# Turning the attention weights of the first two query groups on VectorE and carrying them by DMA, in a stick-breaking decoder block

## The chip, the cores and the metric

The kernel runs on one core of a Trainium2 chip. The metric is the device time of one execution in microseconds, as the median over runs. The profile is of one execution; its own time is given beside its span, which is the stretch from the first to the last instruction. All data is 32-bit floating point. A product of two 32-bit numbers is made from parts: a high part (the number rounded to the format that TensorE multiplies, `float32r`) and a low part (what the rounding left), and of the four products of parts the one of the two low parts is dropped.

## The reference

One decoder layer for one sequence of 1024 tokens and a width of 1024, with 16 heads of 64. What matters here:

```python
h = rms_norm(x, norm_gain) * (1 + scale) + shift           # scale, shift, gate from c
q, k, v, z_a, u, z_b, m_a, m_b = split(h @ w_in)           # 8 x 1024 columns
# stick-breaking attention: key s of query t, s < t
z = q @ k.T * 64 ** -0.5
w = sigmoid(z) * prod_{s < j < t} (1 - sigmoid(z_tj))
attn = w @ v
p_a = (attn * silu(z_a)) @ w_branch_a
p_b = (pool(u) * silu(z_b)) @ w_branch_b                   # window means minus the token
out = rms_norm(x + gate * ((sigmoid(m_a) * p_a + sigmoid(m_b) * p_b) @ w_out))
```

## The kernel before

The sequence is stored backwards, so that the keys a query may see are those after it, and a running product from left to right gives the stick-breaking weights. The program has five stages, one after another: the modulation, the norm and the projection `u`; the values `v` (written to DRAM as `v_d`); the pooling branch with `wzb`, `pool` and `pb`; the attention, with the remaining projections `p` in between; and the end, with `pa` and `o`.

Weights of `w_in` come in tiles of 128 columns: 40 of them belong to the attention stage (`tiles`). Of the first 8 (`PLAIN`) the low part is made where they are used, with the copy on ScalarE and the subtraction on GpSimd. Of the other 32 it is made early by `make_lo` (L129): a load `l_raw`, a copy on ScalarE (L136), a subtraction on VectorE (L137), a store to `wl_d`. `LO_V` and `LO_PB` say how many are made per step of the values and of the pooling branch.

**Attention.** The heads come in 8 pairs `p` of heads `h`; the queries of a head come in 4 groups `t` of 256, each of two blocks `qb` of 128. A unit is (p, h, t); `HT_ORDER` gives the eight units of a pair: t = 0, 2, 0, 2, 1, 3, 1, 3 with h = 0, 0, 1, 1, 0, 0, 1, 1. For one unit:

- `z_items` (L531): for each block of queries, the scores `z` of 128 queries against W = 1024 − 128·qb keys, queries on the partitions, in chunks of at most 512 keys. ScalarE makes `om` (L550) and `be` (L551), GpSimd masks the diagonal (L555), VectorE makes the running product (the scan, L557) and multiplies it into `be` (L558). `be` then holds the weights.
- `turn` (L562): `be` has queries on the partitions, and the product with the values needs keys there. TensorE turns squares of 128 by 128 into a PSUM tile `wt`, up to four at a time (a chunk `kp`), ScalarE copies the high part out (L576), VectorE subtracts for the low part (L577).
- `product` (L580): `avs`, the values times the turned weights, high and low part in turn.
- `finish` (L594): the two halves of the result are added (L602, L603) and multiplied with the silu of z_a on GpSimd (L606), and stored to `ga_d`.

Per pair there are 72 squares to turn. TensorE's order is written out by hand: `step` (L653) deals a unit's product, the scores of the unit three steps ahead (`LEAD`) and 8 or 9 pieces of three `p` products evenly over one step, and TensorE keeps that order. A chunk is turned two chunks ahead of its product (`DEPTH`). The order of the other engines and of the queues is made by a scheduler that plays the program through with costs of its own; once made it is fixed, and an engine that waits for one instruction holds back all that stand behind it. SyncE (SP) issues nearly all DMAs, in its own fixed order. Eight semaphores are dealt round to the DMAs, and a DMA waits until the one before it on its semaphore has landed.

Of the kernel before, what the change touches and what calls it, by code (L numbers as in the profile page):

```python
# [9 lines left out]
F32 = mybir.dt.float32  # L10
# [15 lines left out]
LEAD = {0: 3, 1: 3, 2: 3, 3: 3}  # L26
NBE = (4, 4)
SHARE = (7,) * 8
# [4 lines left out]
BANKS = {"pj": 2, "z": 3, "av": 1, "tr": 2}  # L33
NWT = 4


PLAIN = 8
LO_V = (1, 1, 1, 1, 1, 1, 1, 0)
LO_PB = (1, 1, 1, 1, 1, 1, 2, 2)
HD = 64  # L40
# [8 lines left out]
def block_kernel(ctx, tc, a, out):  # L49
# [66 lines left out]
    def load_w(src, name, hi_eng, lo_eng):  # L116
        raw = wts.tile([P, KB, P], F32, tag="raw", bufs=2, name=name + "_raw")
        nc.sync.dma_start(raw.rearrange("p k c -> p (k c)"), src)
        return split(raw, [P, KB, P], wts, "whl", 2, hi_eng, lo_eng, name)
# [20 lines left out]
    def load_parts(i, name):  # L140
        if i < PLAIN:
            return load_w(a["w_in"][tiles[i]], name, act, gp)
        raw = wts.tile([P, KB, P], F32, tag="raw", bufs=2, name=name + "_raw")
# [42 lines left out]


    early = ExitStack()
    first = early.enter_context(pool("first"))
    with pool("init") as init:  # L190
# [74 lines left out]
        def first_w(i):  # L265
            raw = wts.tile([P, KB, P], F32, tag="raw", bufs=2, name=f"wu{i}_raw")
# [63 lines left out]
    with pool("vp") as vp:  # L330
        def load_wv(hf, k2):
            raw = wts.tile([P, 2, 512], F32, tag="raw", bufs=2, name=f"wv{hf}_{k2}_raw")
            nc.sync.dma_start(raw.rearrange("p k c -> p (k c)"), a["w_v"][hf, k2])
            return split(raw, [P, 2, 512], vp, "wv", 6, act, v, f"wv{hf}_{k2}")
# [31 lines left out]
    with pool("pb") as pb:  # L366
# [4 lines left out]
        for g, win in enumerate(WINDOWS):  # L371
            dhl = []
            for cb in range(2):
# [16 lines left out]
                dhl.append(split(d, [P, S], pb, "dhl", 3, v, v, f"dhl{j}"))  # L390
            praw = wts.tile([P, 2, 256], F32, tag="raw", bufs=2, name=f"praw{g}")
            nc.sync.dma_start(praw, a["pool_w"][g].rearrange("(k p) d -> p k d", p=P))
# [24 lines left out]
        for j in range(KB):  # L417
            sm = [pb.tile([P, 512], F32, tag="zs", bufs=3, name=f"sm{j}_{sh}") for sh in range(2)]
            whl = load_w(a["w_branch_b"][j], f"wb{j}", v, gp)
            wg = wts.tile([P, D], F32, tag="raw", bufs=2, name=f"wg{j}")  # L420
            nc.sync.dma_start(wg, a["w_gate"][j * P:(j + 1) * P, :])
# [17 lines left out]


    with pool("at") as at:
        pair = {}

# [43 lines left out]
        def projections():  # L487
# [7 lines left out]
            todo += gates  # L495
            ws = {}

# [33 lines left out]
        def z_items(u):  # L531

            p, h, t = u
            st = pair[p]
            rows = unit_rows[u] = []
            for qb in (2 * t, 2 * t + 1):
                n0 = qb * P
                W = S - n0
                om = at.tile([P, S], F32, tag="om", bufs=2, name=f"om{p}_{h}_{qb}")
                g = t // 2  # L540
                be = at.tile([P, S - 512 * g], F32, tag=f"be{g}", bufs=NBE[g], name=f"be{p}_{h}_{qb}")
                nch = (W + 511) // 512
                b0 = 0
                for i in range(nch):
# [11 lines left out]
                    if i == nch - 1:  # L556
                        v.tensor_tensor_scan(om[:, :W], om[:, :W], om[:, :W], 1.0, ALU.mult, ALU.min)  # L557
                        v.tensor_mul(be[:, 1:W], be[:, 1:W], om[:, :W - 1])  # L558
                        rows.append(be)
                    yield  # L560

        def turn(u, kp):  # L562

            p, h, t = u
            rows, k0 = unit_rows[u], 2 * t
            pt = bank("tr", f"wt{p}_{h}_{t}_{kp}")
# [13 lines left out]
        def product(u, kp, wt, blocks):  # L580

            p, h, t = u
            vv = pair[p]["vv"]
            if kp == t:
                i = units.index(u) % 2
                avs[u] = av_bank[:, 256 * i:256 * i + 256]
            for j, (kb, o, n) in enumerate(blocks):
                for i in range(2):
                    mm(
                        avs[u][:, :n], vv[:, kb, h].rearrange("p a d -> p (a d)"), wt[:, i, o:o + n],  # L590
                        start=kp == t and j == 0 and i == 0, stop=kp == 3 and j == 1 and i == 1,
                    )

        def finish(u):  # L594
# [9 lines left out]
            if h == 1:  # L604
                sl = slice(t * 256, t * 256 + 256)
                gp.tensor_mul(tp, tp, pair[p]["za"][:, sl])  # L606
                nc.sync.dma_start(ga_d[p][:, sl], tp)
            if (h, t) == HT_ORDER[-1]:
# [75 lines left out]

    with pool("fin") as fin:
        NK = 20

# [140 lines left out]
```

## Time and profile before

| what | value |
|---|---|
| median of 3 runs | 1292.53 us (1291.13 to 1293.98) |
| the profiled execution | 1294.87 us, span 1293.2 us |
| granted TensorE clock, mean | 0.99 |
| TensorE busy | 1241.9 us (96%) |
| VectorE busy | 804.1 us (62%) |
| ScalarE, GpSimd busy | 548.1 us (42%), 279.3 us (22%) |
| moved by DMA | 192.48 MB, mean 149 GB/s |

By the windows and the timeline the stages are: values 137.5 to 224 us; pooling branch to 431.6; attention to 1091, of which pairs 1 to 6 take about 75.4 us each; the end to 1293.2. A busy time is the union of an engine's records, so it hides which wait ends last; the timeline of one engine, with the starts of neighbouring rows, tells what an instruction costs the engine that issues it.

### The profile page before, as it was taken

The numbers are of one execution on the slowest core, as the hardware profiler recorded it, in microseconds if no ns is written. First come the engines' busy times: TensorE is split into PE (matmuls) and PEld (weight loads), VectorE is DVE, ScalarE is ACT, GpSimd is POOL, SyncE is SP. The second block draws the span as 40 slices with busy tenths as digits, with TensorE's granted clock in tenths as the row PEclk, the third lists the DMA queues.
The fourth block names the chain that finished last, engine by engine and source line by source line (L and its number), as shares of the span: only waits on it lengthen the run. The fifth ranks groups of instructions, "written<-read, shape, count | busy, mean of one in ns | idle before, by whom it ended". The sixth has DMA issues, their size and how long they took to land.

```text
span 1293.2 us, 16723 instructions
## 1 busy us (share of the span) xinstructions
PE 1241.9 (96%) x6094; PEld 1035.6 (80%) x6094; DVE 804.1 (62%) x1020; ACT 548.1 (42%) x1029; POOL 279.3 (22%) x397
## 2 busy tenths in 40 slices
PE   6799999989999999999999999999999998889997
PEld 5688888768888888888888888888888887667886
DVE  7915342899611177785877768686776743657654
ACT  4445331231101255565656556565655543312101
POOL 4610000102122332322313122231212211400001
PEclk9899999999999999999999999999999999899999
DMA  8528995862343411233323223232322237855512
GB/s 317 204 98 310 330 343 188 303 225 83 113 146 130 155 42 53 70 114 107 122 77 101 80 98 119 90 122 89 99 72 96 96 107 266 288 186 172 183 65 94
DMA packets 72804, 192.48 MB, mean 149 GB/s; under 512 B 7697, under 2 KB 21009, under 8 KB 70802
## 3 DMA queue, kind: packets, MB, share of 16 engines
q1 hardware_dynamic: 63106, 174.38, 39.4%
q10 hardware_dynamic: 9616, 17.04, 3.9%
q8 instruction: 48, 0.79, 0.2%
q14 instruction: 34, 0.28, 0.1%
HBM read 136.86 MB, written 50.34 MB: 145 GB/s over the span
## 4 chain that ended last, share of the span: by engine, by line
PE 78%; DVE 10%; issue 5%; DMA 4%; ACT 1%; POOL 1%; SPq 0%; POOLq 0%; DVEq 0%; ACTq 0%
PE p L90 30%; PE pb L90 7%; PE v L90 7%; PE avs L90 5%; PE o L90 5%; PE wzb L90 5%; PE z L90 5%; PE wt L90 4%; PE u L90 4%; PE pa L90 4%; DVE acc L234 2%; PE ua L90 1%; PE pool L90 1%; DMA wor<-in_w_out 1%; DVE om L557 1%
## 5 line engine op out<-in xcount | busy, mean ns | idle before, releaser
L90 PE MATMUL p<-hT,w 128*128 128x512 f32 x1920 | 538.2, 401 | 0.0
L90 PEld LDWEIGHTS p<-hT,w 128*128 128x128 f32 x1920 | 335.3, 189 | 45.9 <-issue 0.5
L557 DVE TENSOR_TENSOR_SCAN om<-om 128x512 f32<-128x512 f32 (+7 forms) x128 | 175.7, 1372 | 65.7 <-POOL om L555 41.1
L577 DVE TENSOR_TENSOR wt<-wt,wt 128x512 fp32r<-128x512 f32 (+1 forms) x160 | 101.1, 633 | 66.7 <-ACT wt L576 65.4
L550 ACT ACTIVATE om<-z 128x512 f32<-128x512 f32 (+2 forms) x192 | 94.3, 491 | 112.4 <-PE z L90 109.9
L555 POOL TENSOR_SCALAR_AFFINE_SELECT om<-om 128x128 f32<-128x128 f32 x128 | 62.0, 484 | 354.8 <-ACT om L550 318.1
L576 ACT CAST wt<-wt 128x512 fp32r<-128x512 f32 (+1 forms) x160 | 87.2, 545 | 74.9 <-PE wt L90 71.0
L90 PEld LDWEIGHTS avs<-wt,vv 128*128 128x128 f32 x640 | 96.0, 188 | 18.6 <-DVE tp L603 6.7
L558 DVE TENSOR_TENSOR be<-be,om 128x511 f32<-128x511 f32 (+7 forms) x128 | 102.4, 800 | 11.0
L90 PE MATMUL pa<-ga,wa 128*128 128x512 f32 x384 | 94.6, 402 | 10.9 <-DVE ga L698 3.9
L90 PE MATMUL avs<-wt,vv 128*128 128x256 f32 (+1 forms) x640 | 99.8, 278 | 4.5 <-DVE tp L603 4.5
L90 PEld LDWEIGHTS pa<-ga,wa 128*128 128x128 f32 x384 | 73.4, 194 | 31.0 <-DVE ga L698 5.2
L551 ACT ACTIVATE be<-z 128x512 f32<-128x512 f32 (+2 forms) x192 | 93.5, 487 | 0.0
L90 PE MATMUL wzb<-hT,wzb 128*128 128x512 f32 x384 | 92.2, 396 | 0.0
L90 PE MATMUL o<-wo,mhl 128*128 128x512 f32 (+1 forms) x408 | 89.6, 377 | 2.5 <-DVE mhl L114 2.5
L90 PEld LDWEIGHTS wt<-ident,be 128*128 128x128 f32 x576 | 72.4, 141 | 23.6 <-DVE wt L577 1.7
L90 PE MATMUL wt<-ident,be 128*128 128x128 f32 x576 | 89.1, 272 | 0.8 <-DVE wt L577 0.8
L90 PE MATMUL pb<-gb,wb 128*128 128x512 f32 x384 | 88.1, 391 | 0.0
L90 PE MATMUL v<-wv,hT 128*128 128x512 f32 x384 | 87.2, 389 | 0.0
L90 PEld LDWEIGHTS o<-wo,mhl 128*128 128x128 f32 x408 | 73.3, 188 | 17.3 <-DVE mhl L114 3.3
L90 PEld LDWEIGHTS wzb<-hT,wzb 128*128 128x128 f32 x384 | 73.1, 191 | 16.3 <-DVE zs L400 0.3
L90 PEld LDWEIGHTS pb<-gb,wb 128*128 128x128 f32 x384 | 72.1, 188 | 15.8
(118 smaller groups left out, 1538.9 us busy)
## 6 DMA issues: line engine op xcount, KB each, us to landing
w_raw<-in_w_in SPq DMA_DIRECT2D x40, 512.0 KB, 4.4
l_raw<-in_w_in SPq DMA_DIRECT2D x32, 512.0 KB, 5.5
wl_d<-l_raw SPq DMA_DIRECT2D x32, 512.0 KB, 5.0
w<-wl_d SPq DMA_DIRECT2D x32, 512.0 KB, 3.7
v_d<-vo SPq DMA_DIRECT2D x16, 512.0 KB, 5.3
vv<-v_d SPq DMA_DIRECT2D x8, 1024.0 KB, 5.7
wa_raw<-in_w_branch_a SPq DMA_DIRECT2D x16, 512.0 KB, 4.5
wa<-in_w_mod SPq DMA_DIRECT2D x7, 1024.0 KB, 5.5
```

Source lines behind the costliest of these rows:

```text
L90: ins = op(*args, **kw)
L234: v.scalar_tensor_tensor(acc, wa[:, k], sc[:, k:k + 1], acc, ALU.mult, ALU.add)
L550: act.activation(om[:, b0:b0 + n], zp[:, :n], AF.Sigmoid, scale=-0.125)
L551: act.activation(be[:, b0:b0 + n], zp[:, :n], AF.Sigmoid, scale=0.125)
L555: gp.affine_select(out=tl[:, :P], in_=tl[:, :P], pattern=[[1, P]], compare_op=ALU.is_gt, fill=fill, base=0, channel_multiplier=-1)
L557: v.tensor_tensor_scan(om[:, :W], om[:, :W], om[:, :W], 1.0, ALU.mult, ALU.min)
L558: v.tensor_mul(be[:, 1:W], be[:, 1:W], om[:, :W - 1])
L576: act.copy(wt[:, 0, :off], pt[:, :off])
L577: v.tensor_sub(wt[:, 1, :off], pt[:, :off], wt[:, 0, :off].bitcast(F32))
```

## The change

For units with t = 0 or 1 (`MOVED`) TensorE no longer turns the weights. VectorE turns each `be` in squares of 32 by 32 (one instruction per block of queries, `v.transpose`, 64 in all), into a tile `turned` of which there is one. Sixteen DMAs of 32 partitions each then carry the squares to the partitions where they belong, from SBUF to SBUF, into `moved` (two of them). `take` replaces `turn`: the copy of the high part and the subtraction read `moved` in SBUF instead of PSUM. The columns of `moved` stand in another order, so `product` reads them and writes `avs` with strides, in the same number of products, and the two halves of the result come out swapped, so `finish` multiplies and stores them in two pieces.

The other edits: `PLAIN` is 12 instead of 8, so 28 low parts are made early instead of 32: 8 with the values instead of 14, 12 in the pooling branch instead of 10. The raw weights get pools of their own, with 1 buffer in the attention stage and 2 at the end, where there were 2 throughout; the first two tiles of the attention are loaded ahead of its pool; `wt` has 3 buffers instead of 4, `be` of the turned units 2 instead of 4.

```diff
+NRAW = {1: 2, 2: 1, 3: 2}
+NWT = 3
+MOVED = (0, 1)
-PLAIN = 8
-LO_V = (1, 1, 1, 1, 1, 1, 1, 0)
-LO_PB = (1, 1, 1, 1, 1, 1, 2, 2)
+PLAIN = 12
+LO_V = (1, 0, 1, 0, 1, 0, 1, 0)
+LO_PB = (1, 1, 1, 1, 2, 2, 2, 2)
...
+    first_ws = {i: load_parts(i, f"w{tiles[i]}_{i}") for i in range(2)}
+    rest.close()
     with pool("at") as at:
+        raws.append(at)
...
+            if t in MOVED:
+                nr = 32 * (15 - 4 * t)
+                turned = at.tile([P, 4, 480], F32, tag="turned", bufs=1, name=f"turned{p}_{h}_{t}")
             for qb in (2 * t, 2 * t + 1):
...
                         v.tensor_tensor_scan(om[:, :W], om[:, :W], om[:, :W], 1.0, ALU.mult, ALU.min)
                         v.tensor_mul(be[:, 1:W], be[:, 1:W], om[:, :W - 1])
-                        rows.append(be)
+                        if t in MOVED:
+                            b1 = qb - 2 * t
+                            dst = turned[:, :, :nr].rearrange("p j (b c) -> p b j c", c=32)[:, b1::2]
+                            v.transpose(dst, be[:, :W].rearrange("p (b j c) -> p b j c", j=4, c=32))
+                        else:
+                            rows.append(be)
                     yield
+            if t in MOVED:
+                wm = at.tile([P, 4, 480], F32, tag="moved", bufs=2, name=f"moved{p}_{h}_{t}")
+                for i in range(4):
+                    for j in range(4):
+                        nc.sync.dma_start(wm[32 * j:32 * j + 32, i, :nr], turned[32 * i:32 * i + 32, j, :nr])
+                rows.append(wm)
+
+        def take(u, kp):
+            p, h, t = u
+            off, n = (0, 96) if kp == t else (96 + 128 * (kp - t - 1), 128)
+            wm = unit_rows[u][0]
+            wt = at.tile([P, 2, 4, 128], F32R, tag="wt", bufs=NWT, name=f"wt{p}_{h}_{t}_{kp}")
+            act.copy(wt[:, 0, :, :n], wm[:, :, off:off + n])
+            v.tensor_sub(wt[:, 1, :, :n], wm[:, :, off:off + n], wt[:, 0, :, :n].bitcast(F32))
...
+                    if t in MOVED:
+                        b0 = 2 - n // 32
+                        dst = avs[u].rearrange("p (b i c) -> p i b c", b=2, c=32)[:, :, b0:]
+                        mov = wt[:, i, :, o:o + n].rearrange("p i (b c) -> p i b c", c=32)
```

The change moves instructions on every engine of the attention stage. Three places follow. In the names, the first three numbers behind `om`, `be`, `turned` are pair, head and block of queries (for `turned` and `wt`, the group t); `SCALAR_TENSOR_TENSOR` on `om` is the scan.

**Place A, VectorE.** Head 1 of pair 3 makes its weights for group 0 while the unit (3, 0, 0) waits for its product. Before:

```order
L557 SCALAR_TENSOR_TENSOR om3_1_0_5651<-om3_1_0_5651 128x1024
L558 TENSOR_TENSOR be3_1_0_5652<-be3_1_0_5652,om3_1_0_5651 128x1023
L603 TENSOR_TENSOR tp2_3_5532<-avs_3008,tp2_3_5532 64x256
L557 SCALAR_TENSOR_TENSOR om3_1_1_5696<-om3_1_1_5696 128x896
L558 TENSOR_TENSOR be3_1_1_5697<-be3_1_1_5697,om3_1_1_5696 128x895
L476 TENSOR_TENSOR kl0_3002<-p12_1_5679,kh_4_5589 64x512
L577 TENSOR_TENSOR wt3_0_0_2_5748<-wt3_0_0_2_5743,wt3_0_0_2_5748 128x512
```

With the change:

```order
L570 SCALAR_TENSOR_TENSOR om3_1_0_5702<-om3_1_0_5702 128x1024
L571 TENSOR_TENSOR be3_1_0_5703<-be3_1_0_5703,om3_1_0_5702 128x1023
L648 TENSOR_TENSOR tp2_3_5571<-avs_2998,tp2_3_5571 64x256
L570 SCALAR_TENSOR_TENSOR om3_1_1_5743<-om3_1_1_5743 128x896
L571 TENSOR_TENSOR be3_1_1_5744<-be3_1_1_5744,om3_1_1_5743 128x895
L484 TENSOR_TENSOR kl0_2992<-p12_1_5725,kh_4_5641 64x512 x2
L576 STREAM_TRANSPOSE turned3_1_0_5701<-be3_1_0_5703 128x8x4x32
L576 STREAM_TRANSPOSE turned3_1_0_5701<-be3_1_1_5744 128x7x4x32
L595 TENSOR_TENSOR wt3_0_0_0_5679<-moved3_0_0_5591,wt3_0_0_0_5679 128x4x96
```

Before, the subtractions of chunks 0 and 1 of the unit (3, 0, 0) stand ahead of the first of these rows, and here only that of chunk 2. Now that of chunk 0 stands behind both scans, two subtractions for `kl` and both turns of the next unit.

**Place A, TensorE.** The same place in the order that is written by hand. Before:

```order
L90 MATMUL z3_1_1_1_5724<-kl1_3003,q1_3_5054 128x384
L90 MATMUL p12_1_5679<-hT_88,w12_16_5417 128x512 x6
L90 MATMUL wt3_0_0_2_5743<-ident_77,be3_0_0_5471 128x128
L90 MATMUL wt3_0_0_2_5743<-ident_77,be3_0_1_5512 128x128
L90 MATMUL wt3_0_0_2_5743<-ident_77,be3_0_0_5471 128x128
L90 MATMUL wt3_0_0_2_5743<-ident_77,be3_0_1_5512 128x128
L90 MATMUL avs_3008<-wt3_0_0_0_5631,vv_3_5420 128x256 x2
```

With the change:

```order
L93 MATMUL z3_1_1_1_5771<-kh_3_4896,q1_3_5091 128x384
L93 MATMUL z3_1_1_1_5771<-kl1_2993,q1_3_5091 128x384
L93 MATMUL p12_1_5725<-hT_88,w12_16_5463 128x512 x6
L93 MATMUL avs_2998<-wt3_0_0_0_5679,vv_3_5466 128x4x2x32 x2
L93 MATMUL avs_2998<-wt3_0_0_0_5679,vv_3_5466 128x128 x2
```

The four turns are gone, and six `p` products are what is left between the last scores of (3, 1, 0) and the first product of (3, 0, 0).

**Place C, VectorE.** The unit (2, 1, 1), while pair 3 begins. Before:

```order
L577 TENSOR_TENSOR wt2_1_1_1_5454<-wt2_1_1_1_5450,wt2_1_1_1_5454 128x384
L603 TENSOR_TENSOR tp2_1_5464<-avs_3008,tp2_1_5464 64x256
L577 TENSOR_TENSOR wt2_1_1_2_5489<-wt2_1_1_2_5484,wt2_1_1_2_5489 128x512
L485 TENSOR_TENSOR za_3_5421<-p27_0_5423,za_3_5421 128x512
L557 SCALAR_TENSOR_TENSOR om3_0_0_5470<-om3_0_0_5470 128x1024
L558 TENSOR_TENSOR be3_0_0_5471<-be3_0_0_5471,om3_0_0_5470 128x1023
```

With the change:

```order
L493 TENSOR_TENSOR za_3_5467<-p27_0_5469,za_3_5467 128x512
L570 SCALAR_TENSOR_TENSOR om3_0_0_5513<-om3_0_0_5513 128x1024
L571 TENSOR_TENSOR be3_0_0_5514<-be3_0_0_5514,om3_0_0_5513 128x1023
L648 TENSOR_TENSOR tp2_3_5571<-avs_2998,tp2_3_5571 64x256
L576 STREAM_TRANSPOSE turned3_0_0_5512<-be3_0_0_5514 128x8x4x32
L570 SCALAR_TENSOR_TENSOR om3_0_1_5550<-om3_0_1_5550 128x896
L595 TENSOR_TENSOR wt2_1_1_1_5496<-moved2_1_1_5405,wt2_1_1_1_5496 128x4x96
```

The subtraction of (2, 1, 1) moved from ahead of the scores of (3, 0, 0) to behind both of their scans and one turn.

More of the change, by code (lines that the diff above doesn't have):

```diff
@@ L26 @@
 LEAD = {0: 3, 1: 3, 2: 3, 3: 3}
-NBE = (4, 4)
+NBE = 4
 SHARE = (7,) * 8
@@ L116, in load_w @@
     def load_w(src, name, hi_eng, lo_eng):
-        raw = wts.tile([P, KB, P], F32, tag="raw", bufs=2, name=name + "_raw")
+        raw = raws[-1].tile([P, KB, P], F32, tag="raw", bufs=NRAW[len(raws)], name=name + "_raw")
         nc.sync.dma_start(raw.rearrange("p k c -> p (k c)"), src)
@@ L142, in load_parts @@
             return load_w(a["w_in"][tiles[i]], name, act, gp)
-        raw = wts.tile([P, KB, P], F32, tag="raw", bufs=2, name=name + "_raw")
+        raw = raws[-1].tile([P, KB, P], F32, tag="raw", bufs=NRAW[len(raws)], name=name + "_raw")
         nc.sync.dma_start(raw.rearrange("p k c -> p (k c)"), a["w_in"][tiles[i]])
@@ L185, in copy_out @@
         return use
+    rest = ExitStack()
+    raws = [rest.enter_context(pool("raw"))]
     early = ExitStack()
@@ L265, in first_w @@
         def first_w(i):
-            raw = wts.tile([P, KB, P], F32, tag="raw", bufs=2, name=f"wu{i}_raw")
+            raw = raws[-1].tile([P, KB, P], F32, tag="raw", bufs=NRAW[len(raws)], name=f"wu{i}_raw")
             load(raw.rearrange("p k c -> p (k c)"), a["w_in"][CU + i])
@@ L331, in load_wv @@
         def load_wv(hf, k2):
-            raw = wts.tile([P, 2, 512], F32, tag="raw", bufs=2, name=f"wv{hf}_{k2}_raw")
+            raw = raws[-1].tile([P, 2, 512], F32, tag="raw", bufs=NRAW[len(raws)], name=f"wv{hf}_{k2}_raw")
             nc.sync.dma_start(raw.rearrange("p k c -> p (k c)"), a["w_v"][hf, k2])
@@ L390, in block_kernel @@
                 dhl.append(split(d, [P, S], pb, "dhl", 3, v, v, f"dhl{j}"))
-            praw = wts.tile([P, 2, 256], F32, tag="raw", bufs=2, name=f"praw{g}")
+            praw = raws[-1].tile([P, 2, 256], F32, tag="raw", bufs=NRAW[len(raws)], name=f"praw{g}")
             nc.sync.dma_start(praw, a["pool_w"][g].rearrange("(k p) d -> p k d", p=P))
@@ L419, in block_kernel @@
             whl = load_w(a["w_branch_b"][j], f"wb{j}", v, gp)
-            wg = wts.tile([P, D], F32, tag="raw", bufs=2, name=f"wg{j}")
+            wg = raws[-1].tile([P, D], F32, tag="raw", bufs=NRAW[len(raws)], name=f"wg{j}")
             nc.sync.dma_start(wg, a["w_gate"][j * P:(j + 1) * P, :])
@@ L604, in finish @@
             if h == 1:
-                sl = slice(t * 256, t * 256 + 256)
-                gp.tensor_mul(tp, tp, pair[p]["za"][:, sl])
-                nc.sync.dma_start(ga_d[p][:, sl], tp)
+                n = 128 if t in MOVED else 256
+                for c0 in range(0, 256, n):
+                    c1 = t * 256 + (256 - n - c0)
+                    gp.tensor_mul(tp[:, c0:c0 + n], tp[:, c0:c0 + n], pair[p]["za"][:, c1:c1 + n])
+                    nc.sync.dma_start(ga_d[p][:, c1:c1 + n], tp[:, c0:c0 + n])
             if (h, t) == HT_ORDER[-1]:
```

17 lines of the change are left out of this document (12 added, 5 removed).

## Prediction

> **What bounds the kernel now.** I read the windows by stage first, because a busy share over the whole span mixes stages. The columns are stretch, length, PE busy, PEld, DVE, ACT, POOL, granted clock, DMA share, GB/s. The rows are the values stage, the start of the pooling branch, and pairs 2 and 3 of the attention:
>
> ```profile
> 137.50:222.00 84.50, 84.50 (x375) 69.96 (x374) 32.62 (x35) 26.95 (x33) 5.26 (x18) 1.00 0.83 296
> 250.00:266.00 16.00, 9.02 (x37) 6.29 (x36) 15.97 (x21) 6.00 (x8) 3.26 (x1) 1.00 0.71 235
> 607.00:682.00 75.00, 74.98 (x412) 63.86 (x411) 55.48 (x70) 45.84 (x95) 19.42 (x37) 1.00 0.34 109
> 682.00:757.00 75.00, 74.65 (x410) 63.47 (x409) 55.52 (x70) 44.78 (x94) 18.84 (x36) 1.00 0.30 95
> ```
>
> TensorE is never idle in the values stage and nearly never in the attention (74.98 and 74.65 of 75 us). Only the start of the pooling branch is VectorE's (15.97 of 16 us, TensorE 9.02). So work taken from TensorE in the attention shortens it, as long as nothing there arrives late. VectorE has room by this view: 55.5 of 75 us.
>
> Second, TensorE's timeline, for what a turn costs it (start, length, engine, line, operation, count). Two steps of one pair, each with a group of turns and a gap between two groups of `p` without one:
>
> ```profile
> 614.05 0.60 PE L90 MATMUL wt<-ident,be 128*128 128x128 f32 x4
> 614.40 0.95 PE L90 MATMUL p<-hT,w 128*128 128x512 f32 x3
> 615.19 0.39 PE L90 MATMUL z<-kh,q 128*128 128x512 f32 x1
> ...
> 617.48 0.49 PE L90 MATMUL wt<-ident,be 128*128 128x128 f32 x3
> 617.73 0.94 PE L90 MATMUL p<-hT,w 128*128 128x512 f32 x3
> 618.51 0.64 PE L90 MATMUL avs<-wt,vv 128*128 128x256 f32 x4
> 618.98 0.85 PE L90 MATMUL p<-hT,w 128*128 128x512 f32 x3
> 619.67 0.33 PE L90 MATMUL z<-kh,q 128*128 128x384 f32 x1
> ```
>
> Lengths of neighbours overlap, so I use distances between starts. Three `p` products alone take 619.67 − 618.98 = 0.69 us. With a group of four ahead of them it is 615.19 − 614.05 = 1.14, with three 618.51 − 617.48 = 1.03. A group of four costs 0.45 us, a group of three 0.34. (The records of these turns sum to far more, since they overlap other work.)
>
> **What the change removes.** For t = 0 and 1, a unit has 15 or 11 squares, three in its first group and four in each other: per pair 10 groups of four and 4 of three, 52 of 72 squares. 10 × 0.45 + 4 × 0.34 = 5.86 us per pair, **46.9 us** in 8 pairs. If nothing waited, that would be the gain.
>
> **What it adds on VectorE.** Per pair 2 × (1024 + 896 + 768 + 640) columns to turn, in eight instructions. The trace has no turn on VectorE. Its bounds for 1024 columns are a copy and a scan, and between them lies an operation that gives one result per column:
>
> ```profile
> L114 DVE CAST wzb<-wzb_raw 128x1024 fp32r<-128x1024 f32 x8 | 5.5, 687 | 1.2 <-DMA wzb_raw<-in_w_in 1.2
> L557 DVE TENSOR_TENSOR_SCAN om<-om 128x1024 f32<-128x1024 f32 x16 | 36.7, 2295 | 13.4 <-ACT om L550 12.8 <-POOL om L555 0.5
> L558 DVE TENSOR_TENSOR be<-be,om 128x1023 f32<-128x1023 f32 x16 | 20.3, 1271 | 2.0
> L577 DVE TENSOR_TENSOR wt<-wt,wt 128x384 fp32r<-128x384 f32 x64 | 35.4, 553 | 30.0 <-ACT wt L576 29.6
> ```
>
> The ends are 0.69 and 2.29 us. I take 1.2 for 1024 columns, near the 1.27 of L558, since a turn gives each element once; 1.05 for 896 and 0.9 for 768 in proportion. Per pair that is 3328 × 2 / 1024 × 1.2 = 7.8 us, so VectorE has some 63 us to do while TensorE keeps about 69. **By throughput the change would pay. The order decides otherwise.** The Trainium skill, page "VectorE: DVE Perf Modes", speaks against it twice: § The three transpose paths gives VectorE 311 ns for 128 by 128 and § Rules for kernel authors sends a square of that size to TensorE if PSUM will do. By that figure 1024 columns would take an estimated 8 × 311 = 2.49 us, above the scan of this trace, and the sum below would end near 1349; no run here shows it yet.
>
> **Place A, once in each pair.** The order rows above show the subtraction of chunk 0 of (3, 0, 0) behind both scans and both turns of (3, 1, 0), while TensorE has six `p` products between the last scores of (3, 1, 0) and the products that need this chunk. The same place in the trace of before, on three engines:
>
> ```profile
> 705.63 0.35 PE L90 MATMUL z<-kl,q 128*128 128x384 f32 x1
> 705.81 1.56 PE L90 MATMUL p<-hT,w 128*128 128x512 f32 x6
> 707.21 0.60 PE L90 MATMUL wt<-ident,be 128*128 128x128 f32 x4
> 707.56 0.65 PE L90 MATMUL avs<-wt,vv 128*128 128x256 f32 x4
> ...
> 706.01 0.49 ACT L550 ACTIVATE om<-z 128x384 f32<-128x384 f32 x1 [0.73 <-PE z L90]
> ...
> 706.87 2.02 DVE L557 TENSOR_TENSOR_SCAN om<-om 128x896 f32<-128x896 f32 x1
> 709.03 1.35 DVE L558 TENSOR_TENSOR be<-be,om 128x895 f32<-128x895 f32 x1
> 710.30 0.67 DVE L476 TENSOR_TENSOR kl<-p,kh 64x512 fp32r<-64x512 f32 x1
> 711.00 0.58 ACT L475 CAST kh<-p 64x512 fp32r<-64x512 f32 x1 [0.46 <-DVE kl L476]
> 712.73 0.69 DVE L476 TENSOR_TENSOR kl<-p,kh 64x512 fp32r<-64x512 f32 x1
> ```
>
> Without the turns TensorE could begin the products at 707.21. The chain that must end first runs from the scores: ScalarE is done at 706.50, then scan 2.02, multiplication 1.35, turns 1.20 and 1.05, subtraction 0.55 (L577, same size): 712.67. That is 5.5 us late. In pair 3 both `kl` subtractions (0.67, 0.69) and the copy that the second waits for (0.58) stand in between too: 7.4. In pairs 6 and 7 the rows of the order have one of the two turns ahead: 4.4. In the other five one or two `kl` subtractions stand within the chain, partly in its gaps: 6.0. Mean (7.4 + 2 × 4.4 + 5 × 6.0) / 8 = **5.8 us**, with ends 5.2 (no `kl` counts) and 7.0 (both and the copy count in six pairs). Nothing can cover it: TensorE's order is pinned, so everything behind stands still, the scores of the next units too. That delays their chains equally and gives nothing back.
>
> **Place C, seven times.** The subtraction of (2, 1, 1) stands behind both scans and one turn of (3, 0, 0):
>
> ```profile
> 687.25 0.35 PE L90 MATMUL z<-kl,q 128*128 128x384 f32 x1
> ...
> 688.83 0.60 PE L90 MATMUL wt<-ident,be 128*128 128x128 f32 x4
> ...
> 691.12 0.57 PE L90 MATMUL avs<-wt,vv 128*128 128x256 f32 x4
> ...
> 688.34 2.00 DVE L557 TENSOR_TENSOR_SCAN om<-om 128x896 f32<-128x896 f32 x1
> 690.48 1.09 DVE L558 TENSOR_TENSOR be<-be,om 128x895 f32<-128x895 f32 x1
> ```
>
> The products would begin 0.45 earlier than now, at 690.67. The scan ended at 690.34; with a turn of 1.2 ahead of it and the subtraction behind, 692.09: 1.4 late (pairs 1, 2, 5). In two pairs a subtraction for `za` (0.69 as for `kl`) is in between: 2.1; in two the multiplication instead of it: 690.34 + 1.20 + 1.09 + 0.55 = 693.18, 2.5 late. Mean (3 × 1.4 + 2 × 2.1 + 2 × 2.5) / 7 = 1.9, ends 1.4 and 2.5; I take **1.8**, as VectorE is free of three old subtractions just before.
>
> **Place B, once in each pair.** Products wait already for the sum of the group before:
>
> ```profile
> L90 PEld LDWEIGHTS avs<-wt,vv 128*128 128x128 f32 x640 | 96.0, 188 | 18.6 <-DVE tp L603 6.7
> ```
>
> That addition (L603) stands behind the scan of (p, 0, 1) in VectorE's order, and now behind its turn of 768 columns as well: **0.9 us**, ends 0 (the addition slips ahead) and 1.7 (at the scan's rate).
>
> **The carry.** A moved unit issues 16 DMAs; with eight semaphores the second eight wait for the first. Rows by issue, and one issue on SP:
>
> ```profile
> kh<-kh ACTq DMA_DIRECT2D x32, 128.0 KB, 3.6
> ga_d<-tp SPq DMA_DIRECT2D x32, 128.0 KB, 1.8
> 624.28 0.32 SPq L607 DMA_DIRECT2D ga_d<-tp  x1
> ```
>
> `kh<-kh` is the nearest, SBUF to SBUF. Sixteen issues take 5.1 us, two landings 3.6 (at 1.8) to 7.2 (at 3.6). They overlap, so I estimate the squares 7 to 10 us after the turn. A pair of 75 us has eight steps of 9.4 us; the product comes two steps after the unit's last scores, 18.8 us, of which the chain of place A takes 7, and the subtraction needs them 11 us after the turn or later. So the carry costs 0. That cover is gone at a landing of 6 us: two of them and the last eight issues make 14.6 us, 3.6 too late. SP's other DMAs (`w`, `vv`, `ga_d`) stand behind these sixteen. The loads of weights are issued a tile ahead and lose 5 us of some 19, so 0. The 16 extra `ga_d` stores and multiplications are read only in the end stage: 0.
>
> **The other edits.** In the values stage fewer low parts are made, but TensorE was the bound there, and the work removed ran beside it (VectorE 32.62 of 84.50 us): 0. The pooling branch makes two more, and its start is VectorE's:
>
> ```profile
> L137 DVE TENSOR_TENSOR l_raw<-l_raw,l_hi 128x1024 fp32r<-128x1024 f32 x32 | 39.9, 1245 | 41.4 <-ACT l_hi L136 41.3
> ```
>
> Two of 1.25 us: between 0 (they come in later steps, by `LO_PB`) and 2.5; I take 1. Four tiles more take the GpSimd way in the attention, where POOL is busy 19 of 75 us: 0. The smaller pools let the end's raw weights load later. The last `p` products hide it, and TensorE needs no weights of the end until then:
>
> ```profile
> 1075.74 15.89 PE L90 MATMUL p<-hT,w 128*128 128x512 f32 x69
> ```
>
> 0, with 3 us at most.
>
> **The sum.** 5.8 × 8 + 1.8 × 7 + 0.9 × 8 = 66.2 us of waits against 46.9 saved: +19.3 in the attention, +1 in the pooling branch. From the profiled execution's 1294.87 this is 1315.2. That execution lies 2.3 us above the median of 1292.53, so I forecast **1313 us**, slower by 1.6%. Its own range: low 5.2 × 8 + 1.4 × 7 + 7.2 − 46.9 = +11.7, so 1304; high 7.0 × 8 + 2.5 × 7 + 7.2 − 46.9 + 2.5 + 3 = +39, so 1332.
>
> **The rivals.**
>
> *VectorE runs ahead and place A is absorbed* (faster). It has about 12 us free in each pair. Were the scheduler's order only a tie there, that is, the scan able to start early enough, A would vanish and only C and B stay: 1292.5 − 46.9 + 1.8 × 7 + 0.9 × 8 + 1 = 1266; half of A left gives 1290. For it: the room in the windows. Against it: the scan waits for scores (12.8 of its 13.4 us of idle time stand against ScalarE), and these are on the same pinned TensorE. It decides when A falls below 46.9 − 19.8 = 27 us in the run, 3.4 per pair. Turns at the copy's rate alone take 0.96 from A, 0.5 from C, 0.4 from B, and leave 1299.
>
> *Turns at the scan's rate or above* (slower still). At 2.29 us for 1024 columns A grows by 2.05, C by 1.1, B by 0.8: 16.4 + 7.7 + 6.4 = 30 us, **1343**. For it: crossing partitions may not stream. Against: L557 is the only operation so slow, and it feeds each result back.
>
> *The carry is late.* At a landing of 6 us, 3.6 us late for 32 units is 115 us: beyond 1400. Against it: the two rows above, and DMA queues busy a third of the time here (0.34, 0.30).
>
> *The change does no more than move time* (no change). Waits of 46.9 us equal the saving: A at 3.4.
>
> **Chances.** The forecast, with its range to 1332, 0.62. Slow turns 0.14, late carry 0.04. Absorbed 0.14, no change 0.06. What a measurement of this kernel can tell from no change is 0.2%, 2.6 us. So faster 0.14, same 0.06, slower 0.80. The range for 8 in 10 goes from 1286, a little more than half of A absorbed, to 1350, slow turns with a part of the other upper ends.
>
> **What would show it.** In the profile after: `wt` turns 160 instead of 576; in pairs 1 to 6 a length near 78 us instead of 75.4; TensorE idle at the first `avs` of (p, 0, 0), 5 to 7 us in each pair, put down to ScalarE's copy or VectorE's subtraction of `moved`, with a scan and the turns just ahead of it on VectorE; 1.8 us at (p, 1, 1). Turns of 1.2 us for 1024 columns prove that step, 0.7 or 2.3 another; the issues of `moved` landing within 4 us prove the carry. If place A shows no idle time, the forecast is wrong in its main step. If the idle time stands against a DMA, the carry is.

## The result, and the profile after

The changed kernel takes 1361.96 us (median; 1360.32 to 1363.40) against 1291.87 in the same comparison. The ratio is **1.053, with an interval of 1.051 to 1.055: slower by 70 us**. I had forecast 1313 and a range to 1350. The sign was right, the size was not: 70 us are 3.4 times the 20.5 that I forecast.

The span is 1360.1 us instead of 1293.2. Where the 67 us are, by the first matmul of each stage in TensorE's timeline (for `wzb`, by the load of its first weights):

| stage | before | after | difference | forecast |
|---|---|---|---|---|
| up to the first `wzb` | 224.2 | 222.3 | −1.9 | 0 |
| pooling branch, to the first `p` | 208.5 | 218.2 | +9.7 | +1 |
| attention, to the first `pa` | 658.7 | 722.6 | +63.9 | +19.3 |
| end | 201.7 | 197.0 | −4.7 | 0 |

The attention first. Windows of two pairs of the changed kernel (columns as in the prediction):

```profile
717.90:803.50 85.60, 74.09 (x359) 61.90 (x358) 62.65 (x79) 44.09 (x93) 21.64 (x38) 0.92 0.46 136
888.40:969.80 81.40, 71.12 (x360) 59.82 (x359) 63.56 (x80) 44.71 (x94) 22.15 (x38) 0.96 0.46 139
```

Its group of products, by form (behind the bar busy us and mean ns, then the idle us ahead of it and what ended most of them):

```profile
L93 PE MATMUL avs<-wt,vv 128*128 128x256 f32 x512 | 97.7, 298 | 81.3 <-DVE wt L595 44.8 <-ACT wt L594 19.3 <-DVE tp L648 17.2
```

Three things stand in these rows. The two windows are 86 and 81 us long instead of 75, and TensorE is idle for 11.5 and 10.3 of them. The idle time stands ahead of `avs`, a little over half of it against the subtraction L595, as forecast. And the granted clock, the share of its full clock that TensorE was let have, is 0.92 and 0.96, where the rows of before had 1.00. TensorE lost 52 turns per pair, 5.86 us, and still is busy for 71 to 74 us of a pair. **The third thing was not in my sum at all.**

The turns on VectorE cost what I had put down (1.2, 1.05, 0.9 us):

```profile
L576 DVE STREAM_TRANSPOSE turned<-be 128x1024 f32<-128x1024 f32 x16 | 19.8, 1236 | 3.1 <-DMA moved<-turned 3.0
L576 DVE STREAM_TRANSPOSE turned<-be 128x896 f32<-128x896 f32 x16 | 17.4, 1088 | 0.0
L576 DVE STREAM_TRANSPOSE turned<-be 128x768 f32<-128x768 f32 x16 | 15.5, 971 | 1.0 <-DMA moved<-turned 0.6
L576 DVE STREAM_TRANSPOSE turned<-be 128x640 f32<-128x640 f32 x16 | 13.3, 833 | 0.2
```

Place A in the third pair, from the timelines of four engines (TensorE, VectorE, ScalarE, SP):

```profile
658.74 1.55 PE L93 MATMUL p<-hT,w 128*128 128x512 f32 x6
662.81 0.38 PE L93 MATMUL avs<-wt,vv 128*128 128x256 f32 x1 [2.53 <-ACT wt L594]
666.91 0.90 PE L93 MATMUL avs<-wt,vv 128*128 128x256 f32 x3 [3.71 <-DVE wt L595]
667.61 1.59 PE L93 MATMUL p<-hT,w 128*128 128x512 f32 x3
...
660.42 2.00 DVE L570 TENSOR_TENSOR_SCAN om<-om 128x896 f32<-128x896 f32 x1
...
663.18 1.09 DVE L571 TENSOR_TENSOR be<-be,om 128x895 f32<-128x895 f32 x1
664.19 2.23 DVE L576 STREAM_TRANSPOSE turned<-be 128x1024 f32<-128x1024 f32 x2
666.34 1.72 DVE L595 TENSOR_TENSOR wt<-moved,wt 128x384 fp32r<-128x384 f32 x3
...
662.25 1.55 ACT L594 CAST wt<-moved 128x384 fp32r<-128x384 f32 x3 [1.14 <-DMA moved<-turned]
...
650.24 10.36 SPq L585 DMA_DIRECT2D moved<-turned  x16
```

The chain is the forecast one: scan, multiplication, two turns, and only then the subtraction. But ahead of it stands a wait that I had costed at nothing. The copy of the high part runs only at 662.25: the last of the 16 DMAs was issued at 660.6, and the copy was released by its landing. TensorE was ready at 660.3. So of these 6.2 us of waiting the first 2.5 are the carry's, whatever stood ahead of the subtraction on VectorE; the other 3.7 are the order's. The next three `p` products start 0.46 us apart (1.59 us for three, where 0.85 is usual): they run at half clock.

Windows of 3.4 us on TensorE around this place, and around two other waits, show the clock following the idle time (the first figure behind the length is TensorE's busy time, the third from the end the granted clock):

```profile
622.47:625.88 3.41, 1.55 (x8) 0.99 (x6) 3.41 (x5) 2.63 (x6) 0.92 (x2) 1.00 0.68 198
625.88:629.30 3.42, 2.09 (x13) 1.84 (x14) 3.27 (x6) 0.30 (x1) 1.53 (x2) 1.00 0.09 33
629.30:632.70 3.40, 3.40 (x21) 2.99 (x20) 1.67 (x4) 0.62 (x3) 0.54 (x2) 1.00 0.34 95
...
656.60:660.00 3.40, 3.40 (x19) 2.83 (x17) 3.21 (x4) 2.26 (x6) 1.66 (x3) 1.00 0.40 98
660.00:663.40 3.40, 0.67 (x3) 0.19 (x1) 3.34 (x4) 1.73 (x4) 2.95 (x1) 1.00 0.78 178
663.40:666.80 3.40, 0.00 (x0) 0.00 (x0) 3.40 (x5) 0.40 (x1) 0.00 (x0) 0.51 0.98 355
666.80:670.20 3.40, 3.29 (x9) 2.79 (x10) 1.95 (x4) 0.67 (x2) 0.00 (x0) 0.50 0.93 339
670.20:673.60 3.40, 3.40 (x21) 2.91 (x20) 1.92 (x2) 1.50 (x3) 1.45 (x2) 0.99 0.35 92
...
1096.90:1100.30 3.40, 1.64 (x7) 0.94 (x5) 3.27 (x6) 2.40 (x5) 0.00 (x0) 1.00 0.19 77
1100.30:1103.70 3.40, 3.38 (x11) 2.89 (x11) 2.53 (x4) 1.16 (x3) 0.09 (x1) 0.51 0.32 101
```

A window in which TensorE was busy for 0.67 us is followed by windows at half clock; nine matmuls fit into a window that otherwise takes 21. At 1100 a single wait of 1.8 us (1.64 of 3.4 us busy) was enough. But a wait of 3.2 us that ended at 627.2 lay across two windows, busy for 1.55 and 2.09 us, and the clock stayed at 1.00. The clock's record of this trace changes in steps of 3.41 us. Of its full-clock windows in the attention, all 12 with TensorE busy for less than 1.5 us were followed by half clock, two of the four with 1.55 to 1.67 us, and none with more. So it is not the length of a wait alone that counts, but how much of one window it empties.

The Trainium skill, page "TensorE: Matmul & The Clock Gate", § HAM oscillation — how this bites in real kernels, describes this: a wait of more than some 3.4 us crosses the window by which the clock is set, the clock falls to a half, and the work behind the wait starts slow. The trace agrees on the window and on the half. It differs on the length: here a wait of 1.8 us within one window did it.

**The sum of the attention can now be closed.** I take TensorE's waits from the distances between starts (7.2 us before, 87.7 after; the page's 81.3 counts less, because matmul records overlap). The clock's loss is a half of the time at half clock, 78.5 us in the attention, so 39.3 (the windows of the eight pairs, each by one minus its clock, give 38.7); 8.9 of that fell into the waits, and 30.4 us are left. 658.7 − 46.9 + (87.7 − 7.2) + 30.4 = 722.7; measured were 722.6. So the 46.9 us were saved. Waits took 80.5 (forecast 66.2), and a term that I did not have took 30.4.

By place, all pairs together, in us: A 47.5 (forecast 46.4), C 19.3 (12.6), B 17.2 where 5.9 were before (forecast 7.2 more), (p, 0, 1) 3.8, nearly all of it in one pair (0). At place A about 18 us stand against the copy, which waits for the carry, and 27 against the subtraction (idle time by the profile).

### The profile page after: what moved, and what is told of

Read it like the earlier page. It is cut to its first block, busy times and chain, and to the rows that moved or that the text cites. A ratio compares the mean times of both kernels' runs of the same rounds, so it can differ in the third digit from the quotient of the medians.

```text
span 1360.1 us, 16674 instructions
## 1 busy us (share of the span) xinstructions
PE 1229.5 (90%) x5678; PEld 1016.1 (75%) x5678; DVE 866.2 (64%) x1080; ACT 542.6 (40%) x1025; POOL 314.3 (23%) x417
## 4 chain that ended last, share of the span: by engine, by line
PE 52%; DVE 19%; SPq 10%; DMA 8%; issue 7%; ACT 3%; POOL 1%; DVEq 0%; ACTq 0%; POOLq 0%
PE p L93 14%; SPq L585 9%; PE pb L93 6%; PE v L93 6%; PE o L93 5%; PE u L93 4%; PE pa L93 4%; DVE om L570 4%; PE wzb L93 3%; PE avs L93 3%; DVE turned L576 2%; PE z L93 2%; DVE be L571 2%; DVE wt L595 2%; DVE acc L239 2%
## 5 line engine op out<-in xcount | busy, mean ns | idle before, releaser
L93 PEld LDWEIGHTS p<-hT,w 128*128 128x128 f32 x1920 | 355.7, 196 | 56.8 <-issue 0.5
L93 PE MATMUL avs<-wt,vv 128*128 128x256 f32 (+1 forms) x640 | 110.3, 292 | 81.3 <-DVE wt L595 44.8
L93 PEld LDWEIGHTS avs<-wt,vv 128*128 128x128 f32 x640 | 101.3, 198 | 106.2 <-DVE wt L595 49.2
L568 POOL TENSOR_SCALAR_AFFINE_SELECT om<-om 128x128 f32<-128x128 f32 x128 | 75.0, 586 | 379.0 <-ACT om L563 370.7
L93 PEld LDWEIGHTS wzb<-hT,wzb 128*128 128x128 f32 x384 | 74.5, 194 | 21.1 <-DVE zs L405 4.5
L594 ACT CAST wt<-moved 128x512 fp32r<-128x512 f32 (+1 forms) x112 | 61.8, 590 | 69.1 <-PE avs L93 48.8
L93 PEld LDWEIGHTS v<-wv,hT 128*128 128x128 f32 x384 | 72.1, 188 | 15.0
L595 DVE TENSOR_TENSOR wt<-moved,wt 128x512 fp32r<-128x512 f32 (+1 forms) x112 | 73.0, 681 | 11.9 <-ACT wt L594 11.6
L108 POOL TENSOR_TENSOR wzb<-wzb_raw,wzb 128x1024 fp32r<-128x1024 f32 x8 | 22.9, 2858 | 232.6 <-DVE wzb L117 232.6
```

The lines of the kernel that those rows point to most:

```text
L93: ins = op(*args, **kw)
L108: lo_eng.tensor_tensor(lo, src, hi.bitcast(F32), op=ALU.subtract)
L568: gp.affine_select(out=tl[:, :P], in_=tl[:, :P], pattern=[[1, P]], compare_op=ALU.is_gt, fill=fill, base=0, channel_multiplier=-1)
L594: act.copy(wt[:, 0, :, :n], wm[:, :, off:off + n])
L595: v.tensor_sub(wt[:, 1, :, :n], wm[:, :, off:off + n], wt[:, 0, :, :n].bitcast(F32))
```

## The experiments

The theory at this point: VectorE's order puts the subtraction behind the next unit's chain, which makes the waits; the waits halve TensorE's clock; the low-part edits lengthen the pooling branch. The first rival: the carry is late, and the order does not matter.

**e1, the low parts alone.**

```diff
 # the kernel before
-PLAIN = 8
-LO_V = (1, 1, 1, 1, 1, 1, 1, 0)
-LO_PB = (1, 1, 1, 1, 1, 1, 2, 2)
+PLAIN = 12
+LO_V = (1, 0, 1, 0, 1, 0, 1, 0)
+LO_PB = (1, 1, 1, 1, 2, 2, 2, 2)
```

> The kernel before with the low-part edits alone: PLAIN 12, 8 low parts with the values, 12 in the pooling branch; the turns stay on TensorE. In the changed kernel the stage from the first wzb product to the first p product is 218.2 us long, 208.5 before. If the low parts cause this, this kernel shows about 217 us there, an attention of 659 as before, and some 1300 us in all. Rival: the longer pooling branch comes from something else of the change (the separate pools for the raw weights); then 208.5 us there and 1292 to 1293 in all, as my prediction's +1 would have it.

Measured: 1301.74 us, ratio 1.0065 (1.0046 to 1.0084). The pooling branch takes 214.8 us, the attention 660.0, the end 201.2. So most of the +9.7 (6.3 of it) comes from these edits alone; the seven other runs with these low parts take 215 to 217 us there, so the rest is about what single executions differ by. Windows of the same stretch, first of the kernel before, then of the changed kernel:

```profile
266.00:300.00 34.00, 34.00 (x144) 27.78 (x143) 33.43 (x44) 8.51 (x13) 5.73 (x2) 0.95 0.54 187
```

```profile
266.00:300.00 34.00, 28.27 (x113) 22.32 (x111) 28.57 (x34) 8.23 (x12) 5.17 (x2) 0.93 0.66 224
```

VectorE is not busier after but idler (28.57 instead of 33.43 us), and TensorE with it, while the DMA engines are busier. My price, two subtractions of 1.25 us, was that of the engine's work; what counts in this stretch is a wait. That the loads of `l_raw` end it is likely: in this stage ScalarE's copy waits 22.9 us for them in the changed kernel and 22.5 in e1, against 16.4 before. It was not tested by itself.

**e2, the subtraction on GpSimd.**

```diff
-            v.tensor_sub(wt[:, 1, :, :n], wm[:, :, off:off + n], ...)
+            gp.tensor_sub(wt[:, 1, :, :n], wm[:, :, off:off + n], ...)
```

> The changed kernel with the subtraction of the moved units on GpSimd, so that it no longer stands behind scans and turns on VectorE; the 16 DMAs and the turns are the same. Order theory: TensorE's idle time ahead of the products falls from 87.7 us to 30 to 45, the time at half clock with it from 79 to under 30 us, and the run from 1362 to 1285 to 1310. Carry theory (ScalarE's copy of the high part waits for the squares, so what stands behind it on any engine is late all the same): idle time stays above 70 us and the run above 1345. A GpSimd subtraction should take 0.9 to 1.2 us, by the 2.4 us of 128x1024.

Measured: 1324.44 us, ratio 1.023 (1.020 to 1.027). Waits 66.5 us, the clock's loss 20.6, the attention 692.8. That is between the theories, and no clean test, since GpSimd's subtraction took 1.8 us and slowed VectorE (GpSimd's row, VectorE's multiplication of 895 columns, ScalarE's copy):

```profile
L595 POOL TENSOR_TENSOR wt<-moved,wt 128x512 fp32r<-128x512 f32 x80 | 142.5, 1800 | 6.5 <-ACT wt L594 5.6 <-PE p L93 0.9
L571 DVE TENSOR_TENSOR be<-be,om 128x895 f32<-128x895 f32 x16 | 27.0, 1690 | 1.0
L594 ACT CAST wt<-moved 128x384 fp32r<-128x384 f32 x32 | 16.4, 514 | 27.2 <-DMA moved<-turned 24.7 <-DMA ga_d<-tp 2.4
```

Place C all but went (3.9 us), place A kept 31.5. The copy still waits 24.7 us for the carry. So the order is not the whole cause, and the carry has a part.

**e4, the subtraction ahead of the turns.**

```diff
-            v.tensor_sub(wt[:, 1, :, :n], ...)
+            last[0] = v.tensor_sub(wt[:, 1, :, :n], ...)
...
-                            v.transpose(dst, be[:, :W]...)
+                            with tc.issue_after(last[0].ins):   # order only, no wait
+                                v.transpose(dst, be[:, :W]...)
```

> The changed kernel with each turn ordered behind the last subtraction that was issued before it, nothing else. Order theory: at places A and C up to two turns (2.3 us) no longer stand ahead of the subtraction; the waits fall by some 20 us, the loss by the clock by 5 to 10, the run from 1362 to 1330 to 1340. Carry theory: the subtraction waits for the squares and not for the turns, so the run stays within 1355 to 1370.

Measured: 1328.96 us, ratio 1.027 (1.023 to 1.030). 33 us come back from the order alone, with the same instructions, 30 of them in the attention (692.7 us); I had expected 22 to 32. Waits 66.0, the clock's loss 21.1. Place A falls from 47.5 to 35.8, C from 19.3 to 7.2. What is left ahead of the products stands a third each against the copy, the sum and the subtraction:

```profile
L93 PE MATMUL avs<-wt,vv 128*128 128x256 f32 x512 | 96.7, 296 | 58.5 <-ACT wt L600 19.6 <-DVE tp L654 18.8 <-DVE wt L601 17.7
L600 ACT CAST wt<-moved 128x384 fp32r<-128x384 f32 x32 | 16.4, 513 | 24.1 <-DMA moved<-turned 18.9 <-issue 2.4 <-DMA ga_d<-tp 1.6
```

**e9, the subtraction ahead of the scans too.** The same `issue_after` around the scan in place of the turn.

> The changed kernel with every scan (not every turn, as in e4) ordered behind the last subtraction that was issued before it. It tells a mere mistake of the order from an order that the carry forces. If the scheduler had only misjudged, the subtraction first is right at every place: waits under 45 us, run under 1315. If the squares are really not there yet (16 issues of 0.6 us and a landing of 2.0, 12 us behind the turn), VectorE now stands still at the subtraction until they land, the scans behind it are late, and with them the next units: the run is longer than the changed kernel's, 1370 to 1410, and VectorE's subtraction of moved, by way of the copy ahead of it, waits for the DMAs.

Measured: 1420.94 us, ratio 1.098 (1.094 to 1.102), still a little above what I expected. The attention takes 787.8 us, the waits 129.8. Now the carry is in front everywhere:

```profile
L93 PE MATMUL avs<-wt,vv 128*128 128x256 f32 x512 | 109.7, 317 | 109.4 <-ACT wt L600 84.8 <-DVE tp L654 18.5 <-DVE wt L601 5.8
L600 ACT CAST wt<-moved 128x384 fp32r<-128x384 f32 x32 | 16.4, 511 | 76.9 <-DMA moved<-turned 63.9 <-DMA ga_d<-tp 12.9
```

So the order was only in part a mistake of the scheduler's: ahead of the turns the subtraction gains 30 us in the attention (e4), but ahead of the scans too it holds VectorE up until the squares have landed, and loses 65 (787.8 − 722.6). Order and carry hang together. The squares come 12 us behind their turn, and no place that was tried for the subtraction is free of waits: behind the next unit's chain TensorE waits for it, and ahead of that chain the chain waits for the squares.

**e5, no carry.**

```diff
-                wm = at.tile([P, 4, 480], F32, tag="moved", bufs=2, ...)
-                for i in range(4):
-                    for j in range(4):
-                        nc.sync.dma_start(wm[32 * j:32 * j + 32, i, :nr], turned[32 * i:32 * i + 32, j, :nr])
-                rows.append(wm)
+                rows.append(turned)          # turned has 3 buffers here
```

> The changed kernel without the 512 DMAs: the copy and the subtraction read the tile that VectorE turned, as it stands (three buffers of it), so the squares are on wrong partitions and the attention's values are not the reference's. All turns, copies, subtractions and products are left. The scheduler now has the squares early and puts the subtraction of chunk 0 ahead of the next unit's turns. Order theory: it was the carry's length in the scheduler's own play that pushed the subtraction back; place A falls from 47 us to under 20, all waits from 88 to 25 to 40, the clock loss from 30 to under 10, and the run from 1362 to 1285 to 1305 (the pooling branch keeps its +9). Rival: VectorE has too much to do with the turns themselves; waits stay over 60 us and the run over 1325.

This kernel leaves out the transfers, so its products take squares from the wrong partitions, and only its time is of use. Measured: 1285.24 us, ratio 0.995 (0.993 to 0.996), though VectorE turns as much as in the changed kernel and the pooling branch keeps its loss (216.8 us). Waits 34.1, the clock's loss 10.9, the attention 650.5; place A 8.2, C gone. Subtraction and copy have left the releasers:

```profile
L93 PE MATMUL avs<-wt,vv 128*128 128x256 f32 x512 | 90.4, 289 | 27.0 <-DVE tp L644 26.9
```

The carry, with the order that came with it and the turns' wait for the one `turned` tile, is thus worth 72 us of the attention (722.6 − 650.5). VectorE's turns by themselves leave a gain of 8 us against the 658.7 of before.

**e3 and e6, useless work in the waits.** Ahead of the first product of a unit TensorE does n products of 128x512 that nobody reads, 0.23 us each:

```diff
+FILL = {(0, 0): 16, (1, 1): 6}                  # e3
+FILL = {(0, 0): 26, (1, 1): 10, (1, 0): 9}      # e6
...
+            extra = FILL.get((h, t), 0) if kp == t else 0
+            if extra:
+                ft = bank("tr", f"fl{p}_{h}_{t}")
+                for n_ in range(extra):
+                    mm(ft, h_hi[:, n_ % KB, 0:P], h_hi[:, n_ % KB, 0:512], ...)
```

> The changed kernel with useless products added on TensorE where it waits: 16 of 128x512 ahead of the first product of (p, 0, 0), 6 ahead of that of (p, 1, 1), 0.23 us each, 22 x 8 x 0.23 = 40 us of added work in all. Clock theory: TensorE's clock is halved because it sits idle, 30 us are lost so in the attention; the added products fit into the waits, keep the clock, and the run falls from 1362 to 1340 to 1350 although it does more. Rival (the half clock costs nothing, being hidden in other waits): the run stays at 1362 or rises by up to 40.

> As e3, with 26, 10 and 9 useless products ahead of the first products of (p, 0, 0), (p, 1, 1) and (p, 1, 0): 45 x 8 x 0.23 = 83 us of added work. Clock theory: the waits of 88 us are nearly filled, the loss by the clock falls from 30 to under 10 us, the attention is 658.7 - 46.9 + 90 to 100 = 702 to 712 us, and the run 1340 to 1355, though TensorE does 83 us more than in the changed kernel. Rival: the clock loss hid in the waits; the run rises to 1370 or more.

Measured: e3 1345.60 us, ratio 1.040 (1.037 to 1.043); e6 1335.72 us, ratio 1.034 (1.032 to 1.035). e3 fell into its range, but for less clear a reason than I had given: its attention is only 6.3 us shorter than the changed kernel's, and the clock still loses 23.6 us, since 16 products leave gaps of 2 to 3 us at place A. Of the 14.7 us between the two profiled executions 8.4 lie in other stages, where nothing was added. e6 decides. TensorE does 83 us more than in the changed kernel, and the run is 26 us shorter. Windows of e6, and then the group of the added products:

```profile
466.00:547.00 81.00, 81.00 (x405) 68.31 (x404) 66.76 (x79) 44.46 (x93) 28.82 (x41) 1.00 0.33 91
547.00:628.00 81.00, 76.19 (x392) 64.53 (x391) 65.03 (x75) 43.77 (x92) 34.87 (x42) 1.00 0.37 107
```

```profile
L94 PE MATMUL fl<-hT 128*128 128x512 f32 x360 | 85.6, 389 | 0.0
```

The clock is 1.00 throughout the attention, and that stage takes 702.3 us instead of 722.6. The gain is smaller than the 30.4 us of the clock, because added products and left waits together make 99 us where the waits were 88.

**e7, e8 and e10, a carry that has time.** Only chunks 2 and 3 of the moved units are turned on VectorE and carried; the chunks that a unit's product begins with stay on TensorE. So the carried squares are needed one or two chunks later.

```diff
-                            v.transpose(dst, be[:, :W]...)
+                            v.transpose(dst, be[:, W - 512:W]...)
-                        else:
-                            rows.append(be)
+                        rows.append(be)
...
-            if t in MOVED:
+            if t in MOVED and kp >= 2:
                 return take(u, kp)
 # turned, moved: 256 columns instead of 480; be0: 4 buffers (e10: 3)
 # e8, e10: PLAIN, LO_V, LO_PB as in the kernel before; e10: turned has 2 buffers
```

> A version made for the waits: of the units with t = 0 and 1 only chunks 2 and 3 are turned on VectorE (512 columns of each be) and carried, the chunks before them stay on TensorE; four buffers of be again, turned and moved a half as large. TensorE saves two groups of four per unit, 4 x 2 x 0.45 x 8 = 28.8 us. The first product of a unit needs nothing that was carried, so order theory and carry theory both expect place A nearly gone; what they disagree on is chunk 2, which still comes by DMA. Order theory: waits 15 to 30 us, little loss by the clock, attention 640 to 655, run 1280 to 1298 with the pooling branch's +9. Carry theory: chunk 2 waits instead, waits over 50 us, run over 1310.

> As e7, with the low parts made where the kernel before makes them (PLAIN 8, 14 with the values, 10 in the pooling branch). By e1 this gives back 9 us: 9 less than e7, so 1271 to 1289 by the order theory, under the kernel before. Rival: four more low parts to be loaded in the attention cost there what the pooling branch gains; no difference to e7.

> e8 with two buffers of the turned tile and three of be instead of one and four: a turn no longer waits until the transfers of the unit before have landed. If what is left of the waits in e8 (25 us) hangs on the one buffer, 3 to 8 us less than e8: 1275 to 1280. If it hangs on the additions for the sum (place B, 12 of the 25), no difference to e8's 1283.

Measured: e7 1289.62 us, ratio 0.997 (0.995 to 0.999); e8 1283.25, 0.993 (0.992 to 0.995); **e10 1270.51, 0.982 (0.980 to 0.984), under both kernels**. Waits are 26.3, 24.9 and 19.7 us, the clock's loss 5.1, 3.4 and 0. e7's attention of 655.2 is at the edge of what I expected. e8's gain over e7 is 6.4 us where I expected 9; its pooling branch takes 208.7 us again. In e10 I expected 3 to 8 us less than e8, and 12.7 came. By the profiles 8.6 of them are in the attention; 3.5 stand ahead of the first `wzb`, a stage that takes 221 to 225 us in the runs of this record, whatever the edit. In e8 the turns had waited 9.5 us, 6.7 of it for the transfers of the unit before, and in e10 they wait 0.8: a turn that waits holds up VectorE's whole queue. What is left is the wait for the sum (L645), most of it at place B:

```profile
L93 PE MATMUL avs<-wt,vv 128*128 128x256 f32 x512 | 89.2, 285 | 14.9 <-DVE tp L645 13.9 <-DVE wt L594 0.9
```

One sum holds for all of these runs: 658.7 − 7.2, less 46.9 (28.8 in e7, e8, e10), plus the run's waits, clock loss and added work. (These three are read from the run's own trace, so the sum tests the saving and not what causes the waits.)

| run | waits | clock | added | sum | attention measured |
|---|---|---|---|---|---|
| changed | 87.7 | 30.4 | 0 | 722.7 | 722.6 |
| e2 | 66.5 | 20.6 | 0 | 691.7 | 692.8 |
| e3 | 47.8 | 23.6 | 40.5 | 716.5 | 716.3 |
| e4 | 66.0 | 21.1 | 0 | 691.7 | 692.7 |
| e5 | 34.1 | 10.9 | 0 | 649.6 | 650.5 |
| e6 | 16.2 | 0 | 82.8 | 703.6 | 702.3 |
| e7 | 26.3 | 5.1 | 0 | 654.1 | 655.2 |
| e8 | 24.9 | 3.4 | 0 | 651.0 | 652.5 |
| e9 | 129.8 | 50.9 | 0 | 785.3 | 787.8 |
| e10 | 19.7 | 0 | 0 | 642.4 | 643.9 |

## Why the prediction was right and wrong

- **What bounds the kernel, and what is saved: right.** With 0.45 and 0.34 us a group (46.9 us for 416 turns, 28.8 in e7, e8 and e10) the sums above close within 2.5 us in ten runs.
- **The turns on VectorE: right.** 1.24, 1.09, 0.97 and 0.83 us against 1.2, 1.05 and 0.9. The rival of slow turns (the scan's rate, 1343 us) fell, and with it the estimate of 2.49 us by the Trainium skill, page "VectorE: DVE Perf Modes", § The three transpose paths: the trace has a half of it.
- **Place A: right in sum by luck.** 47.5 us against 46.4. I had put all of it on the order; about 18 us of it are waits of the copy for the carry, which I had at nothing, and the order's own part is about 29 and not 46.
- **Places C and B: mis-sized.** 19.3 instead of 12.6 and 11.3 more instead of 7.2. C also came in the last pair, which I had left out (about 1 us), and took 4.8 us in the first, where the subtraction ran beside one on GpSimd (last section).
- **"So the carry costs 0": wrong.** I took 0.32 us for an issue, the row of `ga_d<-tp`. The trace of the run after has the answer for line L585, the issues as min/median/max in ns and the landings in us:

```profile
L585 SPq DMA_DIRECT2D moved<-turned x512: 507/589/1677, 477.9 to 1133.2; - x171
DMA to landing us min/median/max: 1.8/2.0/5.5
```

  Sixteen issues take 10.4 us, not 5.1; with a landing of 2.0 the squares are there 12 us behind the turn (10.8 to 13.6 in the 32 units), and I had reckoned the subtraction's need at 11. I had bounded the landing from both sides, but not the issue.
- **The step that failed most: the sum.** "Nothing can cover it [...] That delays their chains equally and gives nothing back" stops at the wait. The granted clock stood at 1.00 in the rows that I quoted, and I did not ask what it depends on. A wait at place A is not paid once: the clock stands at half for 3.4 to 10 us from then on. Beyond the waits themselves this is 30.4 of the 44.6 us that my attention is short of, and the rest is waits.
- **The pooling branch: mis-sized,** +9.7 for +1. I had priced the work and not the wait.
- **The end: +0 foreseen, −4.7 measured.** The runs with the separate pools have 191 to 197 us there, e1 and the kernel before, without them, 201.2 and 201.7. No run changed the pools alone, so the cause stays open.
- **The rivals.** "VectorE runs ahead" did not come. The late carry came in part: not as 115 us at a landing of 6 us, but as the copy's wait and as a reason of the order (e5, e9).

## What to carry to other kernels

Price a wait on TensorE with what comes after it: in this trace a window of 3.4 us with TensorE busy for less than 1.5 was followed by half clock every time, and added waits of 80 us cost 111. Where a transfer is put into a pipeline, count its issues at the measured rate of the same kind of transfer, and ask which instruction a scheduler will then push behind which: here a carry of 12 us put a subtraction behind the whole chain of the next unit. If a moved step can be given to the part of the work that is needed last, the same idea that lost 5% can win: here 1.8%.

## What had not been expected of the hardware

- The issue of a DMA from 32 partitions of SBUF to 32 others took 0.59 us on SP (median of 512), with 60 and 44 KB each and also with 32 KB each in e10; that of the `ga_d` store to DRAM 0.32 in the kernel before.
- VectorE and GpSimd can hold each other up. A subtraction of 128x384 on VectorE, 0.51 to 0.65 us in the other 31 cases, took 2.63 beside a GpSimd subtraction:

```profile
555.11 2.52 POOL L108 TENSOR_TENSOR w<-w_raw,w 128x1024 fp32r<-128x1024 f32 x1 [5.59 <-ACT w L113]
555.41 2.63 DVE L595 TENSOR_TENSOR wt<-moved,wt 128x384 fp32r<-128x384 f32 x1
```

  In e2 it shows on both: 1800 ns for 512 columns on GpSimd, and 1690 instead of 1119 for VectorE's multiplication of 895. The Trainium skill, page "SBUF — State Buffer", § Who interferes with whom, says that a VectorE instruction with two SBUF inputs contends with a GpSimd instruction that reads SBUF, for ports that the two engines share under an exclusive lock. These rows agree: the subtraction ended 0.41 us after GpSimd's. The change made such pairs, since the subtraction read PSUM before and now reads SBUF twice.
